# Seven-product pairs in the input projection, wide weight splits and branch results kept in DRAM

## The chip, the cores and the metric

The kernel runs on one core of a Trainium2 chip. The metric is the device time of one execution in microseconds (us). TensorE (PE) multiplies, VectorE (DVE) and ScalarE (ACT) do the elementwise work, GpSimd (POOL) and SyncE (SP) here mostly issue DMAs. The time of the kernel before is the median of three runs, 1539.02 us (1538.18 to 1539.19).

## The reference

One decoder layer on 256 tokens of width 4096, in float32. What takes the time is two large products: the input projection (4096 x 12288) and the output projection (4096 x 4096).

```python
h = rmsnorm(x, ln_g)
proj = h @ w_in
p_x, p_gate, q, k, v, a_gate, s_u, s_gate = jnp.split(proj, _SPLIT_OFFSETS, axis=-1)
y_pool = pool_mixer(p_x, w_pool, pool_scale)
y_attn = stick_breaking_attention(q.reshape(shp), k.reshape(shp), v.reshape(shp))
y_ssm = s5_mixer(s_u, lam_re, lam_im, log_dt, b_re, b_im, c_re, c_im, d_skip, w_glu, b_glu)
# each branch: rmsnorm(y, g) * silu(gate)
y = jnp.concatenate([y_pool, y_attn, y_ssm], axis=-1)
out = rmsnorm(x + y @ w_out, final_g)
```

`s5_mixer` ends in a gated linear unit (GLU), `h @ w_glu` with a 1024 x 2048 matrix.

## The kernel before

**Units and subs.** All weights stream through one list of 528 *subs*. A sub is a 512 KB tile `w`: two row blocks of 128 (slots `2s` and `2s+1`) by 512 columns. Sixteen subs make a *unit*, which gives 512 output columns for all 256 tokens: 24 units of the input projection in the order of `IN_ORDER` (`su`, `px`, `pg`, `sg`, then `v`, `q`, `k` per group of four heads, then `ag`), four GLU units of four subs each, and eight `out` units. The input units `su` to `ag` read the tokens' columns from `xhl`; before the first `out` unit the same tile is filled with the concatenated branch results.

**Three products for one.** A float32 product is made of float32r ones. ACT rounds a tile to `hi`, DVE subtracts to get `lo` (`hi_lo`, line 138), and PE adds up hi·hi, hi·lo and lo·hi (`mm_tok`, lines 235 to 237). A plain sub is 12 matmuls with 512 columns.

**Sevens.** In some subs of the `out` units (`SEVEN`, line 34: five of 16) the 2 x 2 blocks of the sub are multiplied in Strassen-Winograd form: seven block products instead of eight, 21 matmuls with 256 columns (line 183). This needs four sums of weight blocks (`sums_seven`, DVE and ACT), three sums of token blocks per sub (`sums_of_rows`), product banks `pp` beside the unit's accumulator, and a joining step per unit (`join_seven`).

**Order.** SP's queue stands in the order in which the code issues it: loads four subs ahead. On the other engines a scheduler orders instructions by its own estimate of times, program order breaking ties; once built, each engine works its list strictly in order. The code splits two subs ahead of PE, and hands out the mixers' work in steps: three steps of `side_q` after each sub, and `SSM_RATE` steps of the state-space work from sub 30 on. `hi` and `lo` are five 512-column tiles each. The accumulator `pm` has two buffers of two PSUM banks each, so one unit can be read out while the next one is computed.

## Time and profile before

| what | value |
|---|---|
| median of three runs | 1539.02 us |
| the profiled execution, its time | 1538.74 us |
| its span, first to last instruction | 1536.9 us |
| granted TensorE clock, mean | 0.998 |
| PE busy | 1519.2 us, 99% |
| DVE busy | 1185.8 us, 77% |
| ACT busy | 933.0 us, 61% |
| POOL busy | 0.2 us |
| loads of `w`, 512 KB each | 527, median 3.5 us to land |

Busy time is the union of an engine's instructions. A row of a group gives busy time, the mean duration of one, and the idle time of the engine just before them with the engine that ended it. Instructions of one engine overlap at their ends, so the distance from start to start can be shorter than the duration.

### The profile page before, as it was taken

How to read it: one execution, taken by the hardware profiler on the slowest of the kernel's cores; microseconds unless marked ns; L12 is line 12 of the kernel's file. 1: busy time of each engine (PE TensorE's matmuls, PEld its weight loads, DVE VectorE, ACT ScalarE, POOL GpSimd, SP SyncE). 2: the span in 40 equal slices, each digit the busy share in tenths (PEclk: the TensorE clock that was granted, in tenths of full speed). 3: DMA queues.
4: the chain of work that ended last, by engine and by line, in shares of the span. 5: the costliest groups of instructions: out<-in, count | busy, mean ns of one | idle time of the engine just before them, and what ended most of it. 6: DMA issues, size and time to landing. Idle time of an engine off the chain costs nothing.

```text
span 1536.9 us, 21598 instructions
## 1 busy us (share of the span) xinstructions
PE 1519.2 (99%) x7320; PEld 1266.7 (82%) x7320; DVE 1185.8 (77%) x2301; ACT 933.0 (61%) x1677; POOL 0.2 (0%) x4
## 2 busy tenths in 40 slices
PE   8999999999999999999999999999999999999996
PEld 6888788888788887788888888888888888888885
DVE  7579978999899879997556744555678888888886
ACT  7665556666566655575546755456667555555554
POOL 0000000000000000000000000000000000000000
PEclk9999999999999999999999999999999999999999
DMA  9866656565656556544655555545555666666665
GB/s 326 302 231 200 198 171 197 186 207 192 203 192 202 189 164 195 197 167 162 195 188 186 172 191 192 192 157 181 184 190 192 212 218 221 225 209 212 205 217 199
DMA packets 94063, 308.22 MB, mean 201 GB/s; under 512 B 11776, under 2 KB 17664, under 8 KB 93952
## 3 DMA queue, kind: packets, MB, share of 16 engines
q1 hardware_dynamic: 84096, 296.08, 57.5%
q10 hardware_dynamic: 9856, 10.76, 2.4%
q8 instruction: 57, 0.93, 0.2%
q14 instruction: 54, 0.44, 0.1%
HBM read 299.45 MB, written 4.19 MB: 198 GB/s over the span
## 4 chain that ended last, share of the span: by engine, by line
PE 99%; DVE 0%; DMA 0%; ACT 0%; SPq 0%; DVEq 0%; issue 0%; ACTq 0%
PE pm L236 29%; PE pm L235 29%; PE pm L237 29%; PE ps L183 4%; PE pm L183 3%; PE ps_y L556 1%; PE ps_c L652 1%; PE ps_bu L529 1%; PE ps_t L280 0%; PE ps_z L582 0%; PE ps_p L340 0%; PE ps_z L600 0%; PE ps_av L612 0%; PE ps_av L613 0%; DMA xt<-in_xT 0%; PE ps_av L611 0%
## 5 line engine op out<-in xcount | busy, mean ns | idle before, releaser
L82 DVE TENSOR_TENSOR lo<-w,hi 128x512 fp32r<-128x512 f32 (+1 forms) x1048 | 695.4, 677 | 274.1 <-ACT hi L226 267.9
L226 ACT ACTIVATE hi<-w 128x512 fp32r<-128x512 f32 x968 | 602.6, 629 | 459.4 <-PE pm L237 269.7
L235 PE MATMUL pm<-hi,xhl 128*128 128x512 f32 x1872 | 731.4, 391 | 5.9 <-ACT xhl L94 5.9
L236 PE MATMUL pm<-lo,xhl 128*128 128x512 f32 x1872 | 732.9, 392 | 0.0
L237 PE MATMUL pm<-hi,xhl 128*128 128x512 f32 x1872 | 731.3, 391 | 0.0
L235 PEld LDWEIGHTS pm<-hi,xhl 128*128 128x128 f32 x1872 | 352.3, 188 | 79.1 <-ACT xhl L94 5.9
L236 PEld LDWEIGHTS pm<-lo,xhl 128*128 128x128 f32 x1872 | 352.4, 188 | 74.2 <-issue 2.9
L237 PEld LDWEIGHTS pm<-hi,xhl 128*128 128x128 f32 x1872 | 352.1, 188 | 71.4 <-issue 0.8
L91 DVE SCALAR_TENSOR_TENSOR et<-et,pw,tr 128x16 f32<-128x16 f32 (+3 forms) x256 | 55.9, 274 | 0.8 <-ACT tr L94 0.6
L82 DVE TENSOR_TENSOR sums<-t,sums 128x1024 fp32r<-128x1024 f32 x40 | 48.9, 1222 | 9.2 <-ACT sums L94 9.2
L94 ACT ACTIVATE hi<-w 128x256 fp32r<-128x256 f32 x80 | 40.1, 518 | 23.2 <-PE pm L237 18.2
L94 ACT ACTIVATE sums<-t 128x1024 fp32r<-128x1024 f32 x40 | 42.3, 1057 | 19.4 <-DVE t L82 19.3
L94 ACT ACTIVATE tr<-et,pw 128x32 f32<-128x32 f32 (+3 forms) x128 | 45.5, 386 | 8.5 <-DVE et L91 5.7
L183 PE MATMUL ps<-sums,s 128*128 128x256 f32 x240 | 46.5, 283 | 0.0
L82 DVE TENSOR_TENSOR t<-w 128x512 f32<-128x512 f32 x40 | 27.6, 690 | 20.3 <-DMA w<-in_ws 20.1
L544 DVE TENSOR_TENSOR_SCAN tb<-rho,ta 128x256 f32<-128x256 f32 x64 | 40.5, 673 | 0.1
L183 PEld LDWEIGHTS ps<-sums,s 128*128 128x128 f32 x240 | 36.7, 192 | 0.4 <-DVE sums L82 0.2
L82 DVE TENSOR_TENSOR t<-w,t 128x256 f32<-128x256 f32 x80 | 33.5, 419 | 0.3
L94 ACT ACTIVATE sgm<-sgm 128x1024 f32<-128x1024 f32 x24 | 25.2, 1051 | 0.2
L237 PE MATMUL pm<-hi,hhl 128*128 128x512 f32 x64 | 25.2, 394 | 0.0
L236 PE MATMUL pm<-lo,hhl 128*128 128x512 f32 x64 | 25.2, 393 | 0.0
L235 PE MATMUL pm<-hi,hhl 128*128 128x512 f32 x64 | 25.1, 392 | 0.0
(256 smaller groups left out, 1116.2 us busy)
## 6 DMA issues: line engine op xcount, KB each, us to landing
w<-in_ws SPq DMA_DIRECT2D x527, 512.0 KB, 3.5
xsq<-in_xr SPq DMA_DIRECT2D x8, 512.0 KB, 6.8
xr<-in_xr SPq DMA_DIRECT2D x8, 512.0 KB, 4.5
out<-o SPq DMA_DIRECT2D x8, 512.0 KB, 3.9
xt<-in_xT SPq DMA_DIRECT2D x15, 256.0 KB, 6.0
b<-in_bst ACTq DMA_DIRECT2D x16, 192.0 KB, 4.0
u<-uT ACTq DMA_DIRECT2D x96, 32.0 KB, 2.4
fg<-in_fg SPq DMA_DIRECT2D x8, 256.0 KB, 5.8
```

The costliest lines, as they stand in the source:

```text
L82: V.tensor_tensor(o, x, y, op)
L91: V.scalar_tensor_tensor(o, x, s, y, op0, op1)
L94: S.activation(o, x, f, **kw)
L183: T.matmul(o, stat[:, p, :], mov[q], start=begin and k == 0, stop=end and k == 2, skip_group_check=True)
L226: made = S.activation(hi, w[:, kk, :], AF.Copy)
L235: T.matmul(ps[t], stat[:, slot, 0, sl], hi, start=first, stop=False)
L236: T.matmul(ps[t], stat[:, slot, 0, sl], lo, start=False, stop=False)
L237: T.matmul(ps[t], stat[:, slot, 1, sl], hi, start=False, stop=last)
L529: T.matmul(ps[:, c, :], b3r[:, j, c, :], u3r[:, j, :], start=c == 0, stop=True, skip_group_check=True)
L544: V.tensor_tensor_scan(tb[:, c, :], rho[:, pr:pr + 1].broadcast_to([P, L]), ta[:, c, :], 0.0, ALU.mult, ALU.add)
L556: T.matmul(ps[32 * j:32 * j + 32, 0:L], cf[:, j, c, :], ss[j][:, c, :], start=c == 0, stop=c == 1, skip_group_check=True)
L652: T.transpose(ps[:, (c * 2 + t) * P:(c * 2 + t + 1) * P], z[:, t, (h * 2 + c) * P:(h * 2 + c + 1) * P], ident)
```

## The change

Seven-product subs now also stand in the input units (`SEVEN_IN`, three of 16, from the second sub list entry on), and six of 16 in the `out` units, at every second sub from 0 to 10 (`SEVEN_OUT`). That is 71 + 48 = 119 sevens where there were 40. A sub is split as a whole: one `hi` and one `lo` tile of 1024 columns, in a ring of four each; a seven takes two places of the ring, one for three of its raw blocks (768 columns) and one for its four sums, which DVE makes in place in `w`. There is one set of product banks `p7`, and the accumulator has one buffer per token half. The branch results, the attention outputs and the state-space gates leave SBUF: POOL's queue stores them to DRAM and brings some back, and SP's queue loads seven tiles `yk` after the last `ag` unit, where their row sums and their split are now made. The GLU units move behind the second `ag` unit, and the state-space work is handed out at 1.0 instead of 1.5 steps per sub.

```diff
-SUMS_AHEAD = 1
-SEVEN = (2, 5, 7, 9, 11)
+RING = 4
+K4 = 6
+SEVEN_IN = (0, 5, 10)
+SEVEN_OUT = (0, 2, 4, 6, 8, 10)
+REST_AT = 7
...
-SSM_RATE = 1.5
+SSM_RATE = 1.0
...
+    + [("v", V0 + 1536), ("q", Q0 + 1536), ("k", K0 + 1536)]
+    + [("ag", A_G + 512 * i) for i in range(2)]
     + [("glu", n) for n in (1024, 0, 1536, 512)]
-    + [("v", V0 + 1536), ("q", Q0 + 1536), ("k", K0 + 1536)]
-    + [("ag", A_G + 512 * i) for i in range(4)]
+    + [("ag", A_G + 512 * i) for i in range(2, 4)]
...
+    def ring():
+        return [wp.tile([P, 4 * L], F32R, tag=k, bufs=RING, name=k) for k in ("hi", "lo")]
...
+    def split(i):
+        if i < KT // 2:
+            split_x(i)
+        w = wtiles.pop(i).rearrange("p k n -> p (k n)")
+        raw = ring()
+        at = L if seven(i) else 0
+        made = hi_lo(raw[0][:, at:], raw[1][:, at:], w[:, at:])
+        if i == 12:
+            state["gate"] = made.ins.name
+        if seven(i):
+            b12, b11, b22, b21 = (w[:, q * L:q * L + L] for q in range(4))
+            tt(b11, b12, b11, ALU.subtract)
+            tt(b12, b22, b12, ALU.subtract)
+            tt(b22, b22, b11, ALU.subtract)
+            tt(b21, b21, b22, ALU.subtract)
+            sums = ring()
+            hi_lo(sums[0], sums[1], w)
+            htiles[i] = (raw, sums)
+        else:
+            htiles[i] = raw
...
+            (pp[0], xa[:, :, lo_half], b11, begin, False),
+            (pp[1], y[:, 0], t0, False, end),
+            (pp[3], xa[:, :, hi_half], t1, begin, False),
+            (pp[2], y[:, 1], t2, False, end),
+            (ps[0][:, L:2 * L], xb[:, :, lo_half], b21, first, False),
+            (ps[0][:, 0:L], y[:, 2], b22, False, False),
+            (ps[1][:, L:2 * L], xb[:, :, hi_half], t3, first, False),
...
+    def split_x(s):
+        xt = xtiles.pop(s)
+        scales = [ln_g[:, 2 * s + j:2 * s + j + 1] for j in range(2)]
...
+        xs = bp.tile([P, 2, L], F32, tag="xs", bufs=1, name="xs")
+        for j in range(2):
+            act(xs[:, j, :], xt[:, j, :], AF.Copy, scale=scales[j])
...
+        sums_of_x(s, xs)
+        hi_lo(pair[:, :, 0, :], pair[:, :, 1, :], xs)
...
+            if j == 3:
+                G.dma_start(kept[g], t)
...
+    def take_back(g):
+        t = bp.tile([P, 4, L], F32, tag="k4", bufs=K4, name="yk")
+        nc.sync.dma_start(t, kept[g])
+        for h in range(2):
+            s = 2 * g + h
+            if s in SEVEN_OUT:
+                ts7 = bp.tile([P, 3, P], F32, tag="ts", bufs=1, name="ts")
+                row_sums(s, t[:, 2 * h, :], t[:, 2 * h + 1, :], ts7)
+                row_difference(t[:, 2 * h, :])
+        hi_lo(xhl[:, 4 * g:4 * g + 4, 0, :], xhl[:, 4 * g:4 * g + 4, 1, :], t)
...
+    def scaled(ps, name, norm=True):
+        z = bp.tile([P, 2, NU], F32, tag="k4", bufs=K4, name=name)
+        e = state.pop("joined")
+        if norm:
+            times_r(z, ps)
+            times_r(e, [e[:, t, :] for t in range(2)])
...
+        tt(z, z, e, ALU.add)
         return z
...
             if n == 3:
-                for i in range(28):
-                    hi_lo(xhl[:, i, 0, :], xhl[:, i, 1, :], y_src(i))
+                state["s7"], state["n7"] = {}, 0
+                for g in range(7):
+                    take_back(g)
...
         if s == 0:
-            ps = pm.tile([P, 2, NU], F32, tag="pm", bufs=2, name="pm")
-            psl = [ps[:, t, :] for t in range(2)]
+            ps = [pm.tile([P, NU], F32, tag="c%d" % t, bufs=1, name="pm") for t in range(2)]
```

Three places show how DVE's list moves. The rows name output, inputs and shape, with the engines or DMA queues on which the instruction waits.

The first place is DVE in the middle of an `out` unit. Before, between two sevens (`t7` holds the sums of weight blocks, `sums7` their rounded form, `lo` the low part of a plain tile):

```order
L82 TENSOR_TENSOR t7_13118<-w_13108 128x512 [waits DMAHW5_49]
L82 TENSOR_TENSOR lo_13115<-w_13048,hi_13114 128x512 [waits Activation_49]
L82 TENSOR_TENSOR t7_13118<-w_13108,t7_13118 128x256 [waits DVE_49]
L82 TENSOR_TENSOR lo_13140<-w_13077,hi_13139 128x512 [waits DMAHW4_49,Activation_49]
L82 TENSOR_TENSOR t7_13118<-w_13108,t7_13118 128x256 [waits DVE_49]
L82 TENSOR_TENSOR lo_13144<-w_13077,hi_13143 128x512 [waits Activation_49]
L82 TENSOR_TENSOR sums7_13122<-t7_13118,sums7_13122 128x1024 [waits Activation_49]
L82 TENSOR_TENSOR t7_13169<-w_13159 128x512 [waits DMAHW7_49]
```

and now (`lo` of 768 columns are the raw blocks of a seven, the four `w<-w` its sums, the `lo` of 1024 columns from the same `w` their low part, the next one a plain sub):

```order
L89 TENSOR_TENSOR lo_12891<-w_12832,hi_12890 128x768 [waits DMAHW1_49,Activation_49]
L89 TENSOR_TENSOR w_12832<-w_12832 128x256 [waits DVE_49] x4
L89 TENSOR_TENSOR lo_12899<-w_12832,hi_12898 128x1024 [waits Activation_49]
L89 TENSOR_TENSOR lo_12926<-w_12870,hi_12925 128x1024 [waits DMAHW2_49,Activation_49]
L89 TENSOR_TENSOR lo_12944<-w_12888,hi_12943 128x768 [waits DMAHW3_49,Activation_49]
L89 TENSOR_TENSOR w_12888<-w_12888 128x256 [waits DVE_49] x4
L89 TENSOR_TENSOR lo_12952<-w_12888,hi_12951 128x1024 [waits Activation_49]
```

Before, plain subtractions stood between the sums and the low part of the sums; now nothing stands between the fourth sum and the instruction that waits for ACT's rounding of it.

The second place is DVE at the start of the `out` units. Before, the split of the branch results (`xhl<-yaT`) alternates with the plain tiles of the last `ag` unit:

```order
L82 TENSOR_TENSOR xhl_83<-yaT_10407,xhl_83 128x256 [waits PE_49,Activation_49]
L82 TENSOR_TENSOR lo_11492<-w_11445,hi_11491 128x512 [waits DMAHW6_49,Activation_49]
L82 TENSOR_TENSOR xhl_83<-yaT_10407,xhl_83 128x256 [waits PE_49,Activation_49]
L82 TENSOR_TENSOR lo_11496<-w_11445,hi_11495 128x512 [waits Activation_49]
L82 TENSOR_TENSOR xhl_83<-yaT_10407,xhl_83 128x256 [waits PE_49,Activation_49]
```

and now (`agz` is the last `ag` unit's result, `yk` a tile taken back, `ts` and `y7` its row sums):

```order
L89 TENSOR_TENSOR lo_11474<-w_11427,hi_11473 128x1024 [waits DMAHW1_49,Activation_49]
L89 TENSOR_TENSOR agz_11489<-agz_11489,e7_11385 128x1024 [waits Activation_49]
L89 TENSOR_TENSOR ts_11497<-yk_11495 128x128 [waits DMAHW4_49]
L89 TENSOR_TENSOR lo_11603<-w_11445,hi_11602 128x768 [waits DMAHW2_49,PE_49,Activation_49]
L89 TENSOR_TENSOR ts_11497<-ts_11497,yk_11495 128x128 [waits DVE_49]
L89 TENSOR_TENSOR yk_11495<-yk_11495 128x128
L89 TENSOR_TENSOR w_11445<-w_11445 128x256 [waits DVE_49]
L89 TENSOR_TENSOR ts_11497<-yk_11495,ts_11497 128x128 [waits DVE_49]
L89 TENSOR_TENSOR w_11445<-w_11445 128x256 [waits DVE_49] x2
L89 TENSOR_TENSOR xhl_91<-yk_11495,xhl_91 128x4x256 [waits Activation_49]
```

All work on the tiles taken back now stands behind `agz`, which exists only when PE has ended the last `ag` unit.

The third place is DVE at a seven of an input unit while the state-space work runs (`ta`, `tb`, `s` and the scan on line 577 are that work). Before, such work stood between plain tiles:

```order
L82 TENSOR_TENSOR lo_4623<-w_4563,hi_4622 128x512 [waits Activation_49]
L82 TENSOR_TENSOR ta_1022<-ps_bu_4533,et_4418 128x512 [waits DVE_49]
L82 TENSOR_TENSOR tb_1023<-ps_bu_4533,et_4418 128x512 [waits DVE_49]
L82 TENSOR_TENSOR lo_4645<-w_4587,hi_4644 128x512 [waits DMAHW3_49,Activation_49]
L82 TENSOR_TENSOR u3r_4850<-u3_4841,u3r_4850 32x512 [waits Activation_49]
```

and now:

```order
L89 TENSOR_TENSOR w_9158<-w_9158 128x256 [waits DVE_49]
L89 TENSOR_TENSOR ta_1044<-ta_1044,tb_1045 128x256 [waits DVE_49]
L89 TENSOR_TENSOR ta_1044<-ta_1044,tb_1045 128x256
L89 TENSOR_TENSOR w_9158<-w_9158 128x256 [waits DVE_49]
L577 SCALAR_TENSOR_TENSOR tb_1045<-rho_1039,ta_1044 128x256 [waits DVE_49]
L577 SCALAR_TENSOR_TENSOR tb_1045<-rho_1039,ta_1044 128x256
L89 TENSOR_TENSOR w_9158<-w_9158 128x256 [waits DVE_49]
L89 TENSOR_TENSOR ta_1044<-tb_1045,et_8899 128x512 [waits DVE_49]
L89 TENSOR_TENSOR w_9158<-w_9158 128x256 [waits DVE_49]
```

State-space work now also stands between the four sums of one seven.

More of the change, by code (lines that the diff above doesn't have):

```diff
@@ L77, in body @@
     bp = pool("base")
+    up = pool("u")
+    sums_p = pool("sums7")
+    dp = pool("kept", space=bass.MemoryType.DRAM)
     pm = pool("pmain", space=PSUM)
@@ L156, in split_seven @@
[L156 to L168 removed]
+        ui, s = subs[i]
@@ new lines, in seven @@
+        kind = units[ui][0]
+        return s in (SEVEN_OUT if kind == "out" else SEVEN_IN if kind != "glu" and i > 0 else ())
+    def split(i):
[18 more added lines that the diff above has]
+            htiles[i] = raw
@@ L233, in mm_tok @@
+    def mm_tok(ps, stat, slots, pair, first, last, toks=(0, 1)):
+        hi, lo = pair
         for t in toks:
             sl = slice(t * P, t * P + P)
-            T.matmul(ps[t], stat[:, slot, 0, sl], hi, start=first, stop=False)
-            T.matmul(ps[t], stat[:, slot, 0, sl], lo, start=False, stop=False)
-            T.matmul(ps[t], stat[:, slot, 1, sl], hi, start=False, stop=last)
-    state = {}
+            for kk, slot in enumerate(slots):
+                n = slice(kk * NU, kk * NU + NU)
+                begin, end = first and kk == 0, last and kk == 1
+                T.matmul(ps[t], stat[:, slot, 0, sl], hi[:, n], start=begin, stop=False, skip_group_check=True)
+                T.matmul(ps[t], stat[:, slot, 0, sl], lo[:, n], start=False, stop=False, skip_group_check=True)
+                T.matmul(ps[t], stat[:, slot, 1, sl], hi[:, n], start=False, stop=end, skip_group_check=True)
@@ L241, in body @@
+    state = {"s7": {}, "n7": 0}
     xtiles = {}
@@ L654, in channels, with take_u, gen @@
             yield
[L656 to L657 removed]
+    def take_u(z, n):
+        def gen():
             yield from channels(z, uT[:, 4 * n:4 * n + 4, :])
@@ L856, in body @@
                 norm_x()
-                take_u(state.pop("ps0"), 0)
+                z0 = state.pop("z0")
+                times_r(z0, [z0[:, t, :] for t in range(2)])
+                take_u(z0, 0)
         while loaded < min(len(subs), i + 1 + LOAD_AHEAD):
```

306 lines of the change are left out of this document (129 added, 177 removed).

## The prediction

> **What bounds the kernel now.** I read the page's busy times, then the chain that ended last, then PE's waits, then the stages.
>
> ```profile
> PE 1519.2 (99%) x7320; PEld 1266.7 (82%) x7320; DVE 1185.8 (77%) x2301; ACT 933.0 (61%) x1677; POOL 0.2 (0%) x4
> PE 99%; DVE 0%; DMA 0%; ACT 0%; SPq 0%; DVEq 0%; issue 0%; ACTq 0%
> PE pm L235 <- ACT xhl L94: 5.9, 1, 5.9
> PE pm L235 <- DVE o L82: 0.8, 1, 0.8
> ```
>
> TensorE is the bound everywhere: 99% of the chain, 6.7 us of waits in all. DVE's 77% is an average, so I look at stages (start:end, us, then busy time and instructions of PE, PEld, DVE, ACT, POOL, granted clock, DMA share, GB/s): state-space work beside the input projection, a stretch with almost none, the first `out` unit and the second.
>
> ```profile
> 440.00:480.00 40.00, 40.00 (x181) 33.20 (x180) 39.84 (x84) 22.70 (x42) 0.00 (x0) 1.00 0.67 216
> 960.00:1000.00 40.00, 40.00 (x178) 33.14 (x177) 20.42 (x30) 19.50 (x32) 0.00 (x0) 1.00 0.55 185
> 1181.50:1225.30 43.80, 43.76 (x246) 38.24 (x245) 38.66 (x65) 29.47 (x48) 0.00 (x0) 1.00 0.63 207
> 1225.30:1268.00 42.70, 42.70 (x239) 37.34 (x237) 36.49 (x61) 24.74 (x43) 0.00 (x0) 1.00 0.66 219
> ```
>
> DVE is full where the state-space work runs (39.84 of 40) and at 36.5 of 42.7 in an `out` unit. There a little more work, or one bare wait per seven, brings it level with PE. The granted clock is 1.00 throughout, so times convert directly. A 512-column matmul costs 40.0/177 = 0.226 us.
>
> **What PE saves.** The first and last row below enclose 20 seven-matmuls with 256 columns: (1257.09 - 1254.70)/20 = 0.1195.
>
> ```profile
> 1254.70 0.28 PE L183 MATMUL ps<-lo,xhl 128*128 128x256 f32 x1
> ...
> 1257.09 0.40 PE L235 MATMUL pm<-hi,xhl 128*128 128x512 f32 x1
> ```
>
> A seven is 21 x 0.1195 = 2.51 us, a plain sub 12 x 0.226 = 2.71: 0.20 saved. 71 new sevens in input units: **-14.3**. The 8 more in `out` units (-1.6) are inside the figures for those units below.
>
> **What DVE pays in an `out` unit.** Durations of the forms that the change uses, and how such instructions follow each other (timeline: start, us):
>
> ```profile
> L82 DVE TENSOR_TENSOR lo<-w,hi 128x512 fp32r<-128x512 f32 x1008 | 681.1, 687 | 274.0 <-ACT hi L226 267.9 <-DMA w<-in_ws 0.3 <-ACT hi L94 0.2
> L82 DVE TENSOR_TENSOR sums<-t,sums 128x1024 fp32r<-128x1024 f32 x40 | 48.9, 1222 | 9.2 <-ACT sums L94 9.2
> L82 DVE TENSOR_TENSOR t<-w,t 128x256 f32<-128x256 f32 x80 | 33.5, 419 | 0.3
> L82 DVE TENSOR_TENSOR ax<-al,ah 128x768 fp32r<-128x768 f32 x8 | 7.6, 954 | 0.4 <-ACT ah L94 0.3
> L94 ACT ACTIVATE sums<-t 128x1024 fp32r<-128x1024 f32 x40 | 42.3, 1057 | 19.4 <-DVE t L82 19.3
> L94 ACT ACTIVATE ah<-al 128x768 fp32r<-128x768 f32 x8 | 6.7, 836 | 0.8 <-DVE al L91 0.7
> L226 ACT ACTIVATE hi<-w 128x512 fp32r<-128x512 f32 x968 | 602.6, 629 | 459.4 <-PE pm L237 269.7 <-DVE lo L82 155.0 <-DMA w<-in_ws 5.4
> ```
>
> ```profile
> 1264.09 0.68 DVE L82 TENSOR_TENSOR lo<-w,hi 128x512 fp32r<-128x512 f32 x1
> 1264.69 0.88 DVE L82 TENSOR_TENSOR t<-w,t 128x256 f32<-128x256 f32 x2
> 1265.49 0.68 DVE L82 TENSOR_TENSOR lo<-w,hi 128x512 fp32r<-128x512 f32 x1
> 1266.70 1.23 DVE L82 TENSOR_TENSOR sums<-t,sums 128x1024 fp32r<-128x1024 f32 x1 [0.53 <-ACT sums L94]
> 1267.84 0.68 DVE L82 TENSOR_TENSOR lo<-w,hi 128x512 fp32r<-128x512 f32 x1
> ```
>
> ```profile
> 1265.60 1.06 ACT L94 ACTIVATE sums<-t 128x1024 fp32r<-128x1024 f32 x1 [0.85 <-DVE t L82]
> ```
>
> A free instruction starts 0.08 before its forerunner ends (1267.84 against 1267.93). Two dependent 256-column sums take 0.88, which is 0.455 + 0.42, so a dependent one starts 0.03 after the end. From DVE to ACT it is 0.03 (1265.57 to 1265.60), and back 0.04. Above, a plain `lo` covers half of the ACT wait. In the new order nothing stands between the fourth sum and the `lo` that waits. A pair (seven and plain sub) on DVE is then: raw `lo` 0.954 + 0.03, four dependent sums 3 x 0.455 + 0.42 = 1.785, ACT's rounding with both hops 1.12, sums' `lo` 1.14, plain `lo` 1.14 (one 1024-column instruction where two of 0.60 stood): **6.17 us**, against 2.51 + 2.71 = 5.22 on PE.
>
> So PE loses 0.95 per pair as soon as DVE has no lead, and a ring of four places holds little more than one pair. A unit: its first low parts stand behind the last unit's output `o`, two halves of 0.68 with a plain `lo` of 1.14 between, the first begun as its token half ends, some 0.5 ahead of the unit's end; so the second ends 1.95 after the unit's start (an estimate from these rows). Then follow a raw `lo` (2.9), `o` times `fg` (4.0), four sums (5.8), ACT (6.9) and the sums' `lo` (8.0), where PE wants the seven of sub 2 at 5.7. Four pairs more, 4 x 6.17, give 32.7. After it PE still has 10 matmuls of that seven and 59 of five plain subs (one stands ahead), 10 x 0.1195 + 59 x 0.226 = 14.5: **47.2**, +4.5 for each of seven units, **+31.5**. Bounds: PE alone 120 x 0.226 + 126 x 0.1195 = 42.2 (-0.5 each); all of DVE's work in a unit end to end with six bare waits 45.2 (+2.5); no lead at all and the unit's joins exposed 50 (+7). I take the cycle, because each of its links has its row.
>
> The Trainium skill ("VectorE: DVE Perf Modes", section "The DRAIN you can't avoid") says of chained VectorE instructions that "the semaphore costs nothing extra here". By that the sums would follow at 0.34 and a pair take 5.71. The trace's 0.455 speaks against it; it is a rival below.
>
> **The first `out` unit.** All work on the tiles taken back stands behind `agz`, which needs PE's end of the last `ag` unit, E, and an ACT instruction.
>
> ```profile
> L94 ACT ACTIVATE agz<-pm,rtok 128x512 f32<-128x512 f32 x8 | 5.1, 683 | 1.7 <-PE pm L237 1.7
> L82 DVE TENSOR_TENSOR ts<-yaT 128x128 f32<-128x128 f32 x2 | 0.6, 288 | 0.0
> L82 DVE TENSOR_TENSOR s<-ts,s 128x384 fp32r<-128x384 f32 x5 | 2.8, 551 | 0.0
> L91 DVE SCALAR_TENSOR_TENSOR xhl<-ps_t,prm,xhl 128x256 fp32r<-128x256 f32 x4 | 1.9, 478 | 0.5 <-ACT xhl L94 0.5
> ```
>
> From `agz` to the sums' `lo` of sub 10 DVE has 80 instructions: 24 row sums of 0.288, six of 0.551, four of 0.478, five raw `lo` of 0.954, 20 weight sums of 0.419, and 21 of 1024 or 2 x 512 columns at 1.22 (5.1 for the five of `agz`'s gate): 50.0. Less 0.08 each, plus 0.11 for some 17 that wait for the one just ahead: 45.5. With E + 0.8 as the start and two bare waits (2.2): E + 48.5, then PE's 14.5: **63**, +19 against 43.8. Bounds: -1.6, when DVE's lead covers it, and +30, when it also waits for loads `yk` (a 512 KB load lands in 3.5 us) on SP's queue and for stores on POOL's, 0.2 us busy today. I take +19: seven tiles load while `ag` runs, but their work cannot pass `agz` on an in-order engine.
>
> ```profile
> w<-in_ws SPq DMA_DIRECT2D x527, 512.0 KB, 3.5
> ```
>
> **Late sevens in input units.** From a free ring place to the sums' `lo` is ACT 0.84 (768 columns), 0.985, 1.79, 1.12, 1.22 and hops: 6.0 us. PE needs 3 x 2.71 + 0.5 = 8.6 to come there: 2.6 us of slack. But state-space instructions now stand between the sums:
>
> ```profile
> L82 DVE TENSOR_TENSOR s<-ta,tb 128x256 f32<-128x256 f32 x64 | 24.2, 417 | 0.2
> L544 DVE TENSOR_TENSOR_SCAN tb<-rho,ta 128x256 f32<-128x256 f32 x64 | 40.5, 673 | 0.1
> ```
>
> With such durations, 24 of the 71 sevens have more than 2.6 us of it in their chain, 28.5 us beyond in all. PE's own side products in those places give 0.5 to 1.0 us of slack more, which leaves 18 to 10; **+14**. Bounds 0 (DVE ahead throughout) and 28.5. The lower state-space rate is in that count.
>
> **Start and boundaries.** Three `x` pieces are rounded once more before they are split (ACT 0.63, DVE 0.69 ahead of the first product), unit 0 has some 8 us more on DVE under the first loads, and one accumulator and one product bank set make PE wait for the read-out where it was double: **+5**, 0 to 12. The nearest rows are PE's first wait, 5.9, and `agz`, 0.68 for one bank.
>
> **At nothing**: POOL's stores (queue idle), GLU units further back (PE's work, same count), the joins in new order (same count per unit, behind plain subs). Without that cover each store is one landing, 3.5 us.
>
> **Sum**: 1538.7 (profiled; the median is 0.3 above it, 1.8 of it lie outside the span) - 14.3 + 31.5 + 19 + 14 + 5 = **1594**.
>
> **Rivals.**
> 1. PE stays the bound: 1538.7 - 16.0 + 4 for the start = **1527**, faster. For: 6.7 us of waits with 40 sevens, and DVE idle 274 us behind ACT's `hi`, which a list with fewer, wider splits could use. It decides if DVE keeps over 3 us of lead into each seven: an `out` unit is then 42.2, and input sums are never late. Against: the 45.2 that an `out` unit costs DVE alone.
> 2. The cost is only the tiles taken back and late input sums; `out` pairs are carried by DVE's lead from the five plain subs: 1525 + 19 + 14 = **1558**.
> 3. Dependent sums cost no more than free ones: pairs 5.71, units 7.6 + 22.8 + 14.5 = 44.9, seven times 2.3 less, and some 2 less in the first, and chains in input units 0.46 shorter: **1576**. (The Trainium skill's rule named above.)
> 4. In-order waits behind DRAM: 13 waits on stored or loaded tiles at 3.5 to 5 us and the full 28.5: 1594 + 14.5 + 45 = **1650**.
>
> **How the numbers follow.** Forecast 1594: 0.62, own range 1575 to 1615. Rivals: 0.12, 0.13, 0.05, 0.08. Range 1545 to 1635: rival 2 at its centre below, half of rival 4's waits above. A measurement of this kernel can tell about 0.2% (3 us) from no change; 0.03 for that, taken from rival 2's lower edge. Faster 0.12 (rival 1), slower the rest, 0.85.
>
> **What would show it.** PE's waits: a seven's matmuls behind DVE's `lo`, some 30 us in `out` units 2 to 8, some 20 in the first, some 14 in the input units. DVE's idle before `lo` 128x1024, ended by ACT: about 1.1 per `out` seven. `out` units 47 long, the first 63. Matmuls still 0.12 apart. Input units with state-space work as long as before, those without 0.6 shorter. If `out` units are 42 to 43 long, DVE's lead was larger than the ring lets me see; if dependent sums stand 0.34 apart, rival 3; if DVE's largest releaser is a DMA, rival 4.

## The result and the profile after

The changed kernel takes **1663.06 us** (1657.62 to 1664.62, four runs) against 1538.6 us of the kernel before: a ratio of 1.0805, 95% interval 1.0791 to 1.0818. Slower was forecast, but 1594 us (1545 to 1635); more than half of the loss was missed.

Both spans can be cut at PE's first product of a unit (us; units are counted from 1, of which 1 to 28 are the 24 input and 4 GLU units):

| stage | before | after | difference | predicted |
|---|---|---|---|---|
| to the first product | 5.9 | 8.8 | +2.9 | (in the next row) |
| units 1 to 28 | 1175.6 | 1232.5 | +56.9 | -14.3 + 14 + 5 = +4.7 |
| first `out` unit | 43.8 | 63.4 | +19.6 | +19 |
| `out` units 2 to 8 | 300.6 | 342.4 | +41.8 | +31.5 |
| after PE's last product | 11.0 | 14.7 | +3.7 | 0 |
| span | 1536.9 | 1661.8 | +124.9 | +55.2 |

At the end of unit 28 PE waits 4.6 us for the first tile taken back (the last row of the list of waits below). By this cut the wait stands in the row of units 1 to 28; the prediction, which counted from PE's end of the last `ag` unit, had it in the first `out` unit. Counted so, units 1 to 28 grew by some 52 us and the first `out` unit by 24.

The page of the changed kernel, its busy times and its chain by engine:

```profile
PE 1563.6 (94%) x8031; PEld 1312.0 (79%) x8031; DVE 1384.7 (83%) x2336; ACT 934.4 (56%) x1287; POOL 10.5 (1%) x23
...
PE 53%; DVE 25%; issue 8%; DMA 7%; ACT 6%; ACTq 0%; SPq 0%; DVEq 0%; POOLq 0%
```

The chain was 99% PE; now almost half of it is something else, with DVE first. DVE has 199 us more work. PE's waits (us in total, times, longest):

```profile
PE p L197 <- ACT hi L101: 29.0, 24, 9.0
PE pm L228 <- ACT hi L101: 22.1, 52, 0.6
PE p L197 <- DVE lo L89: 11.2, 18, 1.8
...
PE p L197 <- ACT xhl L101: 4.6, 1, 4.6
```

Line 197 is the sevens' matmul: PE waits for the rounded sums (`hi`) and their low part (`lo`). In the whole list one row names the read-out of the accumulator, 0.7 us in all (`pm` behind ACT's `kz`): one accumulator and one bank set cost PE next to nothing. The stages after (columns as in the prediction):

```profile
8.80:1241.30 1232.50, 1192.18 (x6055) 998.00 (x6055) 1052.57 (x1854) 736.30 (x1041) 9.76 (x18) 0.99 0.59 197
1241.30:1304.70 63.40, 51.35 (x254) 44.54 (x255) 53.54 (x89) 34.48 (x42) 0.54 (x1) 0.85 0.50 171
1304.70:1352.90 48.20, 45.42 (x248) 38.19 (x248) 38.74 (x54) 22.42 (x27) 0.00 (x0) 1.00 0.58 191
```

and units 1 to 28 of the kernel before:

```profile
5.90:1181.50 1175.60, 1175.60 (x5417) 967.41 (x5418) 890.30 (x1809) 725.83 (x1325) 0.00 (x0) 1.00 0.59 197
```

DVE in units 1 to 28 went from 890 to 1053 us; and the granted clock, 1.00 before, falls to 0.85 in the first `out` unit. Below, a *stall* is the time by which one main matmul follows another later than 0.23 us (512 columns) or 0.12 us (256), added up. In units 1 to 28, the wait at their end included, it went from 9.7 to 72.4 us.

### The profile page after: what moved, and what is told of

Its sections match the earlier page's. It is cut to its first block, busy times and chain, and to the rows that moved or that the text cites. A ratio compares the mean times of both kernels' runs of the same rounds, so it can differ in the third digit from the quotient of the medians.

```text
span 1661.8 us, 22475 instructions
## 1 busy us (share of the span) xinstructions
PE 1563.6 (94%) x8031; PEld 1312.0 (79%) x8031; DVE 1384.7 (83%) x2336; ACT 934.4 (56%) x1287; POOL 10.5 (1%) x23
## 4 chain that ended last, share of the span: by engine, by line
PE 53%; DVE 25%; issue 8%; DMA 7%; ACT 6%; ACTq 0%; SPq 0%; DVEq 0%; POOLq 0%
PE pm L229 14%; PE pm L228 14%; PE pm L230 13%; DVE lo L89 9%; DVE w L89 5%; ACT hi L101 5%; PE p L197 5%; DMA w<-in_ws 5%; PE pm L197 3%; DVE ta L89 2%; DVE tb L577 1%; DVE et L98 1%; DVE tb L89 1%; DMA xsq<-in_xr 1%; DVE o L89 1%
## 5 line engine op out<-in xcount | busy, mean ns | idle before, releaser
L101 ACT ACTIVATE hi<-w 128x1024 fp32r<-128x1024 f32 (+1 forms) x647 | 634.4, 1013 | 530.7 <-DVE w L89 287.0
L89 DVE TENSOR_TENSOR lo<-w,hi 128x1024 fp32r<-128x1024 f32 (+1 forms) x647 | 742.2, 1172 | 210.9 <-ACT hi L101 209.5
L228 PE MATMUL pm<-hi,xhl 128*128 128x512 f32 x1572 | 596.6, 399 | 30.9 <-ACT hi L101 21.9
L229 PE MATMUL pm<-lo,xhl 128*128 128x512 f32 x1572 | 621.4, 395 | 3.2 <-DVE lo L89 2.9
L230 PE MATMUL pm<-hi,xhl 128*128 128x512 f32 x1572 | 616.9, 393 | 0.0
L89 DVE TENSOR_TENSOR w<-w 128x256 f32<-128x256 f32 x476 | 201.8, 424 | 10.5
L197 PE MATMUL p<-hi,y 128*128 128x256 f32 x476 | 137.9, 301 | 29.1 <-ACT hi L101 29.0
L197 PE MATMUL p<-hi,xhl 128*128 128x256 f32 x476 | 129.6, 287 | 4.6 <-ACT xhl L101 4.6
L197 PE MATMUL pm<-hi,xhl 128*128 128x256 f32 x476 | 131.8, 288 | 0.8 <-ACT kz L101 0.7
L197 PEld LDWEIGHTS p<-hi,y 128*128 128x128 f32 x476 | 93.2, 196 | 40.1 <-ACT hi L101 35.5
L197 PEld LDWEIGHTS p<-hi,xhl 128*128 128x128 f32 x476 | 92.3, 194 | 8.9 <-ACT xhl L101 5.0
L197 PEld LDWEIGHTS p<-lo,y 128*128 128x128 f32 x238 | 46.6, 196 | 24.2 <-DVE lo L89 18.6
L101 ACT ACTIVATE tr<-et,pw 128x32 f32<-128x32 f32 (+3 forms) x128 | 46.2, 387 | 25.0 <-DVE et L98 12.5
```

Of the source, the lines that this page charges most:

```text
L89: V.tensor_tensor(o, x, y, op)
L101: return S.activation(o, x, f, **kw)
L197: T.matmul(o, stat[:, p, :], mov[q], start=start and k == 0, stop=stop and k == 2, skip_group_check=True)
L228: T.matmul(ps[t], stat[:, slot, 0, sl], hi[:, n], start=begin, stop=False, skip_group_check=True)
L229: T.matmul(ps[t], stat[:, slot, 0, sl], lo[:, n], start=False, stop=False, skip_group_check=True)
L230: T.matmul(ps[t], stat[:, slot, 1, sl], hi[:, n], start=False, stop=end, skip_group_check=True)
```

## The experiments

All runs in one table (us). What each edit is and what was expected of it follows, with the run's name in brackets; "..." stands for lines left out.

| run | median | ratio to before | units 1-28 (stall) | first `out` | `out` 2-8 |
|---|---|---|---|---|---|
| changed kernel | 1663.1 | 1.0805 (1.0791-1.0818) | 1232.5 (72.4) | 63.4 | 342.4 |
| in_plain | 1605.4 | 1.0439 (1.0423-1.0454) | 1179.1 (13.3) | 60.1 | 341.1 |
| ssm_last (one run) | 1934.7 | | (34.3) | 60.6 | 341.3 |
| sums_pool | 1678.9 | 1.0921 (1.0905-1.0938) | 1250.7 (91.8) | 60.4 | 340.7 |
| ring4_k5 | 1667.9 | 1.0843 (1.0828-1.0858) | 1233.1 (73.2) | 64.0 | 341.2 |
| ring5_k5 | 1646.7 | 1.0717 (1.0689-1.0744) | 1216.4 (59.5) | 62.6 | 339.9 |
| no_join | 1649.7 | 1.0730 (1.0712-1.0748) | 1218.8 (61.5) | 61.1 | 340.0 |
| no_sums | 1601.0 | 1.0406 (1.0390-1.0421) | 1171.8 (16.4) | 60.7 | 343.0 |
| out_third | 1621.4 | 1.0544 (1.0527-1.0562) | 1228.7 (69.0) | 55.1 | 310.3 |
| out_lo_later | 1645.9 | 1.0707 (1.0690-1.0725) | 1228.8 (69.1) | 64.2 | 327.3 |
| out_cover | 1613.2 | 1.0500 (1.0483-1.0518) | 1227.3 (68.8) | 60.7 | 298.3 |
| back_early | 1651.9 | 1.0742 (1.0726-1.0758) | 1230.6 (70.6) | 55.2 | 340.8 |
| mix1 | 1547.0 | 1.0058 (1.0043-1.0073) | 1178.3 (12.5) | 43.8 | 300.6 |
| mix2 | 1542.5 | 1.0030 (1.0018-1.0041) | 1177.0 (11.1) | 46.4 | 298.3 |
| mix2_in1 | 1569.9 | 1.0206 (1.0192-1.0220) | 1202.3 (34.5) | 49.1 | 298.3 |

### The pair in an `out` unit

The chain of waits of the changed kernel inside the second `out` unit (start, us, what) shows the cycle that was forecast:

```profile
1325.52 2.10 DVE lo L89 x2
...
1327.64 0.44 DVE w L89
1328.08 0.02 issue
1328.10 0.43 DVE w L89
...
1328.56 0.43 DVE w L89
...
1329.02 0.44 DVE w L89
...
1329.56 1.07 ACT hi L101
...
1331.80 1.22 DVE lo L89
```

PE isn't in it: low parts, four dependent sums, ACT's rounding, low parts again, 1331.80 - 1325.52 = 6.28 us for a pair that PE multiplies in 5.22.

**Fewer sevens per unit** (out_third).

```diff
-SEVEN_OUT = (0, 2, 4, 6, 8, 10)
+SEVEN_OUT = (0, 3, 6, 9, 12)
```

> Five sevens per out unit, at every third sub (0, 3, 6, 9, 12) where six stood at every second. Theory (the pair costs DVE 6.17 us against 5.22 on PE): a seven and two plain subs cost DVE 6.17 + 1.14 = 7.3 against 7.93 on PE, so PE is the bound again: out units 2 to 8 at 42.5 where they took 48.1 to 50.0, minus 45 in all, and the first a few us shorter: 1613 (1605 to 1625). Rival (a fixed cost at each unit's start, behind the output's subtraction and its fg product): units at 46, 1640.

Six of the seven units took 43.9 to 44.2 us, one 46.6: 310 instead of 342, total 1621. With two plain subs per seven DVE (7.3 us by the prediction's rows) is again shorter than PE. The theory held; 1.2 us of stall per unit, at its first two sevens, is what it left out.

**The sums' low part behind the next plain sub** (out_lo_later; rounding and low part of a seven's sums are emitted with the next sub, and ordered behind its own):

```diff
...
-            hi_lo(sums[0], sums[1], w)
             htiles[i] = (raw, sums)
+            if units[subs[i][0]][0] == "out":
+                state["low"] = (sums, w)
+            else:
+                hi_lo(sums[0], sums[1], w)
         else:
             htiles[i] = raw
+            if "low" in state:
+                sums, w = state.pop("low")
+                hi_lo(sums[0], sums[1], w, state["last"])
```

> Same sevens, but in out units the rounding and the low part of a seven's sums stand behind those of the next plain sub, so that 1.14 us of DVE work covers ACT's 1.06. Theory (bare wait): a pair costs DVE 5.05, PE's 5.22 is the bound, units 43 to 45 with their start: total 1663 - 30 = 1633 (1620 to 1645); DVE's idle time before the 1024-column low part behind ACT falls from about 1.1 per seven to under 0.3. Rival (the ring of four: the plain sub's place comes free only at the end of the pair before, and now holds up the sums too): a pair stays at 6.2 or more, total 1655 to 1675.

Measured 1645.9, between the two. DVE's timeline shows why:

```profile
1409.08 3.23 DVE L89 TENSOR_TENSOR lo<-w,hi 128x1024 fp32r<-128x1024 f32 x3 [1.21 <-ACT hi L101]
1412.23 1.80 DVE L89 TENSOR_TENSOR w<-w 128x256 f32<-128x256 f32 x4
1415.23 3.23 DVE L89 TENSOR_TENSOR lo<-w,hi 128x1024 fp32r<-128x1024 f32 x3 [1.21 <-ACT hi L101]
```

The scheduler put the plain low part ahead of the four sums, not behind them. The pair still has its bare wait of 1.21 us and takes 1415.23 - 1409.08 = 6.15 us (in the changed kernel 6.28, by the prediction 6.17). Only the unit's start became shorter. The edit didn't do what it was for, so a second one followed.

**The same, with the plain low part held behind the fourth sum** (out_cover):

```diff
...
+                sums, w, fourth = state.pop("low")
+                plain = state["last"]
+                behind(plain[1], fourth)
+                hi_lo(sums[0], sums[1], w)
+                for one, other in zip(state["last"], plain):
+                    behind(one, other)
```

> The run with the sums' low part behind the next plain sub left a pair at 6.15 us: its order has the plain low part ahead of the four sums, so that nothing stands between the fourth sum and the low part that waits for ACT, 1.21 us. Here the plain low part is held behind the fourth sum too. Theory (the bare wait is what makes a pair longer than on PE): DVE's pair is 5.05, PE's 5.22 bounds: out units 2 to 8 at 42.5 to 44, total 1646 - 20 = 1626 (1618 to 1634), DVE's idle time there behind ACT's rounding under 0.3 per seven. Rival (ring of four: ACT may round the sums only when the pair before has left PE, so the wait moves from DVE's to ACT's list): pairs at 5.8 or more, total 1640 to 1665.

Measured 1613.2, better than expected. `out` units 2 to 8 take 42.6 us each without any stall. One of them by engine, then DVE's group of 1024-column low parts in these seven units (busy, mean ns, idle time ahead of it), in this run:

```profile
1296.90:1339.50 42.60, 42.60 (x247) 37.60 (x246) 39.09 (x55) 22.97 (x27) 0.00 (x0) 1.00 0.65 220
```

```profile
L89 DVE TENSOR_TENSOR lo<-w,hi 128x1024 fp32r<-128x1024 f32 x110 | 133.2, 1220 | 12.1 <-ACT hi L101 9.5
```

and the same group in the changed kernel:

```profile
L89 DVE TENSOR_TENSOR lo<-w,hi 128x1024 fp32r<-128x1024 f32 x111 | 131.6, 1222 | 61.8 <-ACT hi L101 61.8
```

DVE does the same work (39 us per unit) in 42.6 instead of 48.9 us. 61.8 us of waiting for ACT's rounding fell to 9.5, and PE is the bound. So the whole loss of the pair was one wait that nothing covered. It was not DVE's load, and not the ring of four places, which the other theory named.

### The first `out` unit

**The tiles from DRAM taken back in the course of the last `ag` unit** (back_early):

```diff
...
-                for g in range(7):
-                    take_back(g)
...
+        if kind == "ag" and nth.get("ag") == 3 and s % 2 and s < 14:
+            take_back(s // 2)
```

> The tiles that come back from DRAM are loaded, summed and split in the course of the last ag unit, each after PE has used its slots, where all of it stood behind agz. Theory (first out unit 63 because 80 DVE instructions stand behind agz): the first out unit falls from 63.4 to 47 to 52, the ag unit ahead of it grows by 0 to 4, total 1663 - 12 = 1651 (1645 to 1657). Rival (the DRAM traffic itself is late: a load that waits for its store on SP's queue holds up the weights behind it): the stall moves into the ag unit, total over 1658.

55.2 instead of 63.4 us, the `ag` unit ahead 1.3 longer, total 1651.9. The direction held; the unit came out 3 us above the range given for it, and behind the tiles the same pair wait remains: in mix2 and mix1, which have both edits and no input sevens, it is 46.4 (six sevens) and 43.8 (five, as long as before the change). In the changed kernel the wait is not all DVE's own work. Its timeline there has a hole:

```profile
1254.83 0.29 DVE L89 TENSOR_TENSOR ts<-yk 128x128 f32<-128x128 f32 x1
1257.85 1.41 DVE L98 SCALAR_TENSOR_TENSOR ya<-ya,r_b,agz 128x512 f32<-128x512 f32 x2 [2.73 <-DMA ya<-kept_a]
```

A POOL load of an attention output, issued only at 1251.84 and 6.0 us on its way, held DVE for 2.7 us, with the sums of sub 4 queued behind it, for which PE waited 9.0 us (the longest wait of the list above).

### The input units

**No sevens there** (in_plain):

```diff
-SEVEN_IN = (0, 5, 10)
+SEVEN_IN = ()
```

> Input units without sevens; the out units, the DRAM tiles and the wide splits stay. In the changed kernel units 1 to 28 (24 input, 4 GLU) took 1232.5 us against 1175.6 before, out units 405.7 against 344.5. Theory (late sevens: DVE carries some 2.8 us more per input seven and stands in order behind state-space work, both ahead of the raw low part and between the sums): without them those units are back at 1178 to 1188 though PE has 14.3 us more to do; total 1663 - 50 = 1613 (1603 to 1623). Rival (the wide splits, the one accumulator and bank set or the DRAM traffic slow the input units): they stay above 1215, total above 1640.

Units 1 to 28 are back at 1179.1, the total at 1605.4. So the sevens had cost 53.4 us net of what PE saves by them. The 3.5 us that are left are the wait for the first tile taken back: unit 28 takes 48.6 us where it took 44.4, and the other 27 together 0.7 less than before. So the wide splits, the stores to DRAM, the single accumulator and the later GLU units together cost nothing there.

**The state-space work in one piece ahead of the GLU units** (ssm_last):

```diff
-SSM_RATE = 1.0
+SSM_RATE = 0.0
```

> No state-space steps are handed out during the input units; all of that work is done in one piece ahead of the GLU units, which makes the total much longer (1850 to 2000) and is not the question. The question is the stage before: input units 2 to 21. Theory (state-space work on DVE makes the sevens late): their PE stalls, 56 us together in the changed kernel, fall under 10, and a unit without side products takes 43 to 44. Rival (the seven's own chain through the ring is too long, with or without other work): stalls stay above 30.

(The units meant are 3 to 22 by the count used here.) Their stalls fell from 54.4 to 13.7 us, 10.7 of them in the last one, in which the piece begins. Units 8 to 18, with three sevens each, run without a gap:

```profile
337.30:843.00 505.70, 505.70 (x2654) 435.39 (x2653) 350.02 (x421) 284.24 (x326) 2.67 (x5) 1.00 0.58 190
```

So a seven's chain fits through the ring when the state-space work is out of DVE's list. A unit without side products takes 43.0 us here and 43.5 in the kernel before: 0.5 us for three sevens, near the 0.60 of the prediction.

What is late with state-space work shows in the last of these units of the changed kernel, on DVE:

```profile
1058.45 0.94 DVE L89 TENSOR_TENSOR lo<-w,hi 128x768 fp32r<-128x768 f32 x1
...
1059.97 0.42 DVE L89 TENSOR_TENSOR w<-w 128x256 f32<-128x256 f32 x1
...
1060.97 0.42 DVE L89 TENSOR_TENSOR w<-w 128x256 f32<-128x256 f32 x1
...
1062.05 0.42 DVE L89 TENSOR_TENSOR w<-w 128x256 f32<-128x256 f32 x1
...
1063.65 0.42 DVE L89 TENSOR_TENSOR w<-w 128x256 f32<-128x256 f32 x1
1063.98 0.16 DVE L98 SCALAR_TENSOR_TENSOR r_b<-rs_t,r_b 128x2 f32<-128x2 f32 x1
1064.05 0.76 DVE L89 TENSOR_TENSOR ta<-ta,tb 128x256 f32<-128x256 f32 x2
1064.72 1.42 DVE L98 SCALAR_TENSOR_TENSOR ya<-ya,r_b,agz 128x512 f32<-128x512 f32 x2
1066.05 1.28 DVE L577 TENSOR_TENSOR_SCAN tb<-rho,ta 128x256 f32<-128x256 f32 x2
1067.23 2.35 DVE L89 TENSOR_TENSOR lo<-w,hi 128x1024 fp32r<-128x1024 f32 x2
```

and on PE:

```profile
1065.28 0.39 PE L197 MATMUL p<-hi,y 128*128 128x256 f32 x1 [0.85 <-ACT hi L101]
1066.23 0.49 PE L228 MATMUL pm<-hi,xhl 128*128 128x512 f32 x1 [0.44 <-ACT hi L101]
1068.50 0.39 PE L197 MATMUL p<-lo,y 128*128 128x256 f32 x1 [1.77 <-DVE lo L89]
```

From the raw low part to the sums' low part it is 8.8 us, where the seven alone needs 3.9 (0.985 + 1.785 + 1.12). State-space work, a norm of 128x2 values and the gate of an attention branch stand in between. This is the mechanism that the prediction named, with more in the chain than it counted. Five further runs ask why it cost so much more.

**The four sums on POOL** (sums_pool):

```diff
-            tt(b11, b12, b11, ALU.subtract)
+            add = V if units[subs[i][0]][0] == "out" else G
+            add.tensor_tensor(b11, b12, b11, ALU.subtract)
```
(and the other three likewise)

> In input units POOL makes the four weight sums of a seven, on out units DVE as before. DVE loses 284 instructions, about 1.7 us per input seven, but the chain of a seven gets two more engine changes. No run so far has elementwise work on POOL. Theory (input sevens are late through DVE's load and order, not through the length of their chain): with POOL under about 1.1 us per sum the 54 us of stalls in units 3 to 22 fall under 20, total 1620 (1605 to 1635). Rival (the chain's length decides; POOL over 1.5 us per sum, or slows DVE beside it): no gain, total 1655 to 1700.

Slower, 1678.9: the rival. POOL's rows, and one of DVE's that doesn't belong to the sevens, in this run:

```profile
L169 POOL TENSOR_TENSOR w<-w 128x256 f32<-128x256 f32 x71 | 67.9, 956 | 886.0 <-DVE lo L89 824.0 <-DMA u<-uT 23.1 <-DMA w<-in_ws 22.8
...
L172 POOL TENSOR_TENSOR w<-w 128x256 f32<-128x256 f32 x71 | 57.4, 809 | 5.5
```

```profile
L89 DVE TENSOR_TENSOR s<-ta,tb 128x256 f32<-128x256 f32 x64 | 35.9, 600 | 0.6
```

A sum takes 0.81 to 0.96 us there, twice DVE's 0.42, so the chain is some 1.6 us longer; and DVE's own `s<-ta,tb` rose from 0.422 in the changed kernel to 0.600 us on the mean. The Trainium skill ("SBUF — State Buffer", "SBUF: two separate sides") says that a GpSimd instruction that reads SBUF and a VectorE one with two SBUF inputs exclude each other. These rows agree, and so does `ta<-ps_bu,et`, which has one of its inputs in PSUM and stayed as it was (0.687 and 0.682). The sums were 121 us of DVE's work, but as other instructions grew, DVE's busy time in units 1 to 28 fell by 32 us only (1052.6 to 1020.6). So the run shows that POOL is no place for the sums, and doesn't separate DVE's load from the length of the chain.

**A fifth place in the ring** (ring5_k5; paid with one working tile of 4 KB less and two shared places), and the same payment without the place (ring4_k5):

```diff
-RING = 4
-K4 = 6
+RING = 5
+K4 = 5
```

> The changed kernel with five places in the ring for hi and lo instead of four (paid with five working tiles of 4 KB instead of six, and two small tiles in shared places). By its order 29 of the 71 input sevens have more than 2.6 us of other DVE work between the raw low part and the sums' low part, 54 us beyond that bound together; beyond 5.3 us there are 4. Theory (lead: a fifth place gives each seven a plain sub more, 2.7 us): the 72 us of stalls in units 1 to 28 fall below 35, and out pairs gain little, since a pair costs DVE 6.15 in any ring: total 1663 - 40 = 1623 (1610 to 1640). Rival (load: DVE has no time left in those stretches, so a longer ring only shifts the wait): above 1650.

> The same working tiles as the kernel with five places, but four places: what the five working tiles cost by themselves. Expected within 5 us of the changed kernel, 1658 to 1668; if it is far above, the gain of the fifth place is the difference to this run.

1646.7 against 1667.9: the place is worth 21 us, 17 of them in units 1 to 28, where the stall fell only from 73.2 to 59.5 and not under 35. 2.7 us more lead should have covered nearly all of the work found between the sums, so many chains must start late. The expectation was wrong here, and the rival (load) nearer. One reason that neither names stands in ACT's list, at the rounding of the sevens' raw blocks, first with four places and then with five (units 1 to 28):

```profile
L101 ACT ACTIVATE hi<-w 128x768 fp32r<-128x768 f32 x73 | 61.7, 845 | 62.9 <-DMA w<-in_ws 35.8 <-PE pm L230 16.4 <-DVE ta L89 2.8
L101 ACT ACTIVATE hi<-w 128x768 fp32r<-128x768 f32 x73 | 61.6, 844 | 56.7 <-DMA w<-in_ws 41.5 <-PE pm L230 5.1 <-DVE e L89 2.2
```

With the fifth place the wait for PE, which frees a place, fell by two thirds, but the wait for the load of `w` didn't. In all of ACT's roundings of `w` there, the waits for loads come to 118 us in ring5_k5, 116 in ring4_k5, 100 in the changed kernel, 7 without the sums (no_sums, below) and 2 without sevens. There are four tiles `w`, and a seven now keeps its own until the sums' low part is made, so a late chain also delays the loads. No run gives `w` a fifth tile; what that would bring stays open.

**The joins left out (no_join), and the sums left out (no_sums)**, in input units only:

```diff
-                state["joined"] = join_seven(pp)
                 if kind == "out":
+                    state["joined"] = join_seven(pp)
```

> The changed kernel without the joining step in the 24 input units: the products in the banks are not added to the unit's result, so the output lacks them. DVE loses 24 x (4 x 0.42 + 1.22) = 70 us, ACT 24 x (0.41 + 2 x 0.63) = 40 us; PE does the same. Theory chain (a seven is late by what stands between its raw low part and its sums' low part; by the order this stays at 52 us beyond the bound, against 54): stalls in units 1 to 28 stay at 65 or more, total within 12 of 1663. Rival (DVE's load as such: each us taken off counts): stalls fall by 20 or more, total 1640 or less.

```diff
+            if units[subs[i][0]][0] == "out":
-            tt(b11, b12, b11, ALU.subtract)
+                tt(b11, b12, b11, ALU.subtract)
```
(and the other three likewise)

> The changed kernel without the four weight sums in input units: the raw blocks are rounded in their place, so the output is not the reference's. DVE loses 71 x 1.79 = 127 us, and each chain 1.79 us and the places in which other work stands: by the order only 2 of 71 sevens keep more than 2.6 us of it, 1.4 us beyond. Theory chain: stalls in units 1 to 28 fall from 72 to 15 to 25, total 1663 - 50 = 1613 (1605 to 1622). Rival (load: 127 of the 212 us that the sevens add on DVE there, so about six tenths of the loss of 57): total 1663 - 34 = 1629 or more.

The joins are worth 13.7 us in units 1 to 28 (stall 72.4 to 61.5), between the two theories. The sums are worth 60.7, more than the 53.4 that the sevens had cost net of PE's saving; with 1601.0 the total is below the range of either theory:

```profile
9.10:1180.90 1171.80, 1165.60 (x6055) 986.39 (x6055) 952.10 (x1569) 742.31 (x1041) 9.77 (x18) 1.00 0.63 207
```

DVE still has 952 us here, 112 more than without sevens (840), yet PE stalls for 16 us only. DVE's load alone doesn't decide: mix2_in1 (below) has 956 us there and stalls for 34.5. Leaving out the joins took 53.0 us off DVE's busy time in this stage (1052.6 to 999.6), leaving out the sums 100.5; per us that is 13.7/53.0 = 0.26 and 60.7/100.5 = 0.60. The difference fits the place of the sums in the chain, four dependent instructions with the work that the scheduler lays between them. But no run shortens the chain and leaves DVE its load, so how much of the 60.7 is the one and how much the other is not shown.

### Towards a better kernel

mix1 joins in_plain, out_third, out_cover and back_early. mix2 has six sevens per `out` unit again, and holds PE's order in the last four subs:

```diff
+            half = state["mm"]
             for s, pair, last in delayed:
-                mm_tok(ps, xhl, (2 * s, 2 * s + 1), pair, False, last, (1,))
+                mm_tok(ps, xhl, (2 * s, 2 * s + 1), pair, False, last, (1,), half)
```

> Sum of what was learned: no sevens in input units, five per out unit at every third sub, the sums' low part behind the next plain one, the tiles from DRAM taken back in the course of the last ag unit. From the run without input sevens (1605): out units 2 to 8 from 341 to 7 x 42.8 = 300, the first from 60 to 47: 1551 (1543 to 1560), so still slower than before, whose units 1 to 28 and whose end were 3.5 and some 4 us shorter. Rival: the gains don't add (first unit or SP's queue holds): 1565 or more.

> The combined kernel (no input sevens, covered sums, early tiles) again with six sevens per out unit, and with PE held to end the first token half before it begins the second half of the last four subs. In the changed kernel the scheduler mixed the two halves, so the 4 MB of output begin only after PE's end: 15.8 us from PE's end to the end of the span in the combined kernel, 11.0 before. Theory: out units 42.6 instead of 42.9 (minus 2), the end minus 3.5: 1541 (1537 to 1545), level with before or up to 0.5% above it. Rival (the end is set by the stores themselves, wherever they begin): 1544 to 1547.

mix1 took 1547.0, mix2 1542.5, both as expected: the gains of the edits add up. mix2 is still 0.3% slower than the kernel before (interval 0.18 to 0.41%). Its `out` units 2 to 8 are faster than before (298.3 against 300.6), but the first one (46.4), units 1 to 28 (+1.4) and the start (+1.1) take more than that back.

The edit on the last subs answers the 3.7 us at the end of the table of stages. In mix1, as in the changed kernel, DVE's two halves of the last output come close together:

```profile
1528.78 0.69 DVE L90 TENSOR_TENSOR o<-pm,xr 128x512 f32<-128x512 f32 x1 [2.60 <-PE pm L249]
1529.91 0.69 DVE L90 TENSOR_TENSOR o<-pm,xr 128x512 f32<-128x512 f32 x1 [0.44 <-PE pm L249]
```

In the kernel before:

```profile
1519.34 0.69 DVE L82 TENSOR_TENSOR o<-pm,xr 128x512 f32<-128x512 f32 x1 [1.07 <-PE pm L237]
...
1525.89 0.69 DVE L82 TENSOR_TENSOR o<-pm,xr 128x512 f32<-128x512 f32 x1 [1.56 <-PE pm L237]
```

There the first token half is ready 6.5 us earlier and is stored while PE does the second. In the changed kernel, where the accumulator is two tiles, the scheduler mixed the halves. With the order held, the stretch after PE's end is 11.3 us in mix2 (15.8 in mix1).

**One seven per input unit** (mix2_in1):

```diff
-SEVEN_IN = ()
+SEVEN_IN = (5,)
```

> The combined kernel with six sevens per out unit (1542.5), and one seven per input unit (sub 5) in place of none: 24 instead of the change's 71. Each saves PE 0.20 if its sums are in time, 4.8 together. By its order 10 of the 24 have more than 2.6 us of other DVE work in their chain, 16.6 beyond that bound. Theory (what makes them late is work of the state-space stretches, so also single ones are late there): 1542.5 - 4.8 + 12 to 17 = 1552 (1547 to 1558). Rival (with a third of the sevens DVE has the time, and is ahead): 1538 (1536 to 1541), level with before or under it.

1569.9, worse than either theory: 24 sevens cost 25 us in units 1 to 28, 1 us each, and 2.7 in the first `out` unit. DVE has 956 us of work in units 1 to 28, mix2 850: 106 more for 24 sevens, or 4.4 each, where the 71 of the changed kernel cost it 212 (1053 less the 840 of in_plain), 3.0 each. Every unit now pays its join for a single seven. Late sums of sub 5 and one longer wait in the last `ag` unit (5.4 instead of 2.2) are part of it, and ACT's roundings of `w` waited 56 us for loads in units 1 to 28 (6 in mix2); how the 25 us divide stays open.

## Why the prediction was right and wrong

- **What PE saves: right.** ssm_last has units of 43.0 us without side products, 0.5 below before (predicted 0.6), and 42.6 in `out` units once nothing else is in the way. Where the sums are late, none of it arrives.
- **The pair in `out` units: right in mechanism and size.** 6.28 us on DVE against 6.17 predicted, 0.98 of stall per pair against 0.95. out_cover shows that this wait is the whole of it. The term +31.5 came out as +41.8: the first two sevens of a unit cost some 2 to 3 us where the prediction's sum leaves 47.2 - 42.2 - 4 x 0.95 = 1.2, and in two units PE's clock fell (2.7 us, below).
- **The first `out` unit: right in mechanism, some 5 us short; that 63 and 63.4 agree is luck.** The prediction counted from E, PE's end of the last `ag` unit (1236.6), and the 63.4 begin with the unit's first product at 1241.3, for which PE had waited. From E the unit ended after 68 us, not 63, and the low part of sub 10's sums after 53.4, not 48.5. back_early shows that the place behind `agz` made it long. The price for DRAM (rival 4) was real too, but small: one load held DVE for 2.7 of these 5 us. PE's products there also took 6.8 us longer at half the clock; how much of that its waits would have hidden is open.
- **Late sevens in input units: the step that failed.** "24 of the 71 sevens have more than 2.6 us of it in their chain, 28.5 us beyond in all ... **+14**", with bounds of 0 to 28.5. In place of +14 stand 53.4 us by which the sevens made these units longer (in_plain), and 14.3 more that PE saved meanwhile: 68 us. The mechanism was right: in_plain, ssm_last and no_sums each remove the loss. The term was too small for four reasons, which overlap. Only state-space work was counted; by the built order all DVE work between raw and sums' low part comes to 54 us beyond the slack, on 29 sevens. The slack was counted as if a chain began as soon as its ring place was free; ring5_k5 shows that a place more is worth 17 us only, and that ACT then still waits for loads of `w`. The joins were set at nothing as "same count per unit", though 24 units have them that had none: 13.7 us (no_join). And the late sevens brought PE's clock down: 8.4 us in these units (last section).
- **Start and boundaries: mixed.** The first product came 2.9 us later, and unit 1 took 3.0 us longer (49.3 against 46.3), near the +5. The single accumulator and bank set cost 0.7 us by the list of waits.
- **At nothing:** right for the stores, the wide splits and the later GLU units (in_plain), wrong for the joins. The end of the program, +3.7, stands in no term of the sum; mix2, which holds PE's order there, has most of it back (11.3).
- **Rivals.** 1 (PE stays the bound) is what out_cover makes of the `out` units and ssm_last of the input units, so its condition was stated rightly, and not met. 2 (DVE's lead carries the pairs) fell with the stall of 0.98 us per pair. 3 (dependent sums as cheap as free ones) fell: the four sums take 1.80 us as a block, 3 x 0.46 + 0.42; the rule that the prediction quoted from the Trainium skill ("VectorE: DVE Perf Modes", "The DRAIN you can't avoid") does not hold for these chains. 4 named 1650 (its own sum gives 1653.5) and came nearest in number, but for another reason: by its own sign DVE's largest releaser would be a DMA, and it is ACT's `hi`.

## What to carry to other kernels

A block that one engine makes and another rounds must have other work standing between its last instruction and the one that waits, in the order as built. Check that order, since an edit in the program that should move it may not: out_lo_later left a wait of 1.2 us per pair that out_cover removed, worth 33 us. When work is added to an engine that is full in some stretches, count everything that stands in and ahead of the new chain, not the main competitor alone, look at every buffer that the chain holds (here the tile `w` as well as the ring), and count steps per unit that become steps in more units. Saving 0.2 us of the bounding engine per instruction group is worth trying only where the group's operands are sure to be early: in mix2_in1, late, each cost 1 us.

## What was not expected of the hardware

Short stalls can cost more than their length: PE's granted clock fell to one half after some of them. In the changed kernel, around the first late seven of unit 2, and in `out` unit 3 (columns as above, the eighth is the granted clock):

```profile
58.10:62.10 4.00, 2.05 (x14) 1.65 (x13) 3.04 (x5) 3.53 (x6) 0.00 (x0) 1.00 0.20 60
62.10:65.50 3.40, 3.40 (x15) 3.01 (x14) 3.17 (x3) 2.15 (x4) 0.00 (x0) 0.51 0.40 123
...
1359.10:1362.60 3.50, 2.06 (x13) 1.53 (x12) 2.30 (x3) 2.74 (x3) 0.00 (x0) 1.00 0.00 0
1362.60:1366.00 3.40, 3.40 (x13) 2.81 (x12) 2.73 (x6) 0.42 (x1) 0.00 (x0) 0.50 0.85 255
```

In both cases PE was busy for little more than half of the stretch ahead (two gaps of 1.07 and 0.88 us in the first), then ran 3.4 us at half the clock, with matmuls of 512 columns 0.43 us apart instead of 0.23:
```profile
64.21 0.63 PE L228 MATMUL pm<-hi,xhl 128*128 128x512 f32 x1
64.64 0.63 PE L229 MATMUL pm<-lo,xhl 128*128 128x512 f32 x1
...
65.76 0.39 PE L229 MATMUL pm<-lo,xhl 128*128 128x512 f32 x1
65.99 0.39 PE L230 MATMUL pm<-hi,xhl 128*128 128x512 f32 x1
```

After the first 5 to 6 us of products, which all three run at half the clock, the changed kernel has 11 such stretches, 47.8 us together, in which its matmuls took some 18 us longer: 8.4 in units 1 to 28, 6.8 in the first `out` unit, 2.7 in the others; mix2 and the kernel before have none. A gap of 0.6 us per pair, as in most `out` units, did not bring it on. The Trainium skill ("TensorE: Matmul & The Clock Gate", "What's actually happening") gives the half clock after an idle window of about 3.4 us. The length of the slow stretches agrees with that, and two of the eleven (at 1239.7 and 1260.2) begin within waits of 4.6 and 9.0 us. But ahead of the other nine PE was busy for 0.9 to 2.0 of the last 3.4 us, so here a whole idle window was not needed. How short a stall does no harm, these runs don't settle. The prediction's "times convert directly" held for the kernel before only, and each late seven was priced without this.
